# Decoder layer with mixture of experts: low halves of the down weights and routing weights made on VectorE in place of GpSimd

## The chip, the cores and the metric

The kernel runs on one core of one Trainium2 chip. The metric is the device time of one execution in microseconds (us), by the median of several runs. In the text PE is TensorE, DVE is VectorE, ACT is ScalarE, POOL is GpSimd and SP is SyncE, which here only issues DMA loads. L1710 is line 1710 of the kernel before; in the changed kernel lines after L1659 stand one lower (L1711).

## What is computed

One decoder layer for 1024 tokens of 1024 float32 values: attention by two mixers, attention over a memory, and a mixture of 16 experts, of which each token uses 2. The change is in the last of these:

```python
combine = jnp.sum(jax.nn.one_hot(expert_id, N_EXPERTS, dtype=jnp.float32) * w_sel[..., None], axis=-2)
y = jnp.zeros(h.shape, jnp.float32)
for e in range(N_EXPERTS):
    act = jax.nn.silu(h @ w_gate[e]) * (h @ w_up[e])
    y = y + combine[..., e:e + 1] * (act @ w_down[e]).astype(jnp.float32)
return y.astype(h.dtype)
```

`w_gate` and `w_up` are 1024 x 256 per expert, `w_down` is 256 x 1024. The kernel computes only the rows that an expert was chosen for.

## The kernel before

Matmuls are exact to about float32 by halves: every operand is split into a high half (made on ACT, `hi`) and a low half (`lo` = operand minus `hi`), and `mm3` (L520 to L522) adds three products, hi x hi, hi x lo and lo x hi. So each weight tile costs one ACT instruction and one subtraction for its halves before PE can use it.

Before the experts, the rows of all tokens are scattered in DRAM into a table `d_xs`, sorted by expert, with four extra values per row (two routing weights, an expert's number, the token). `moe` then goes over the experts in the order of their size, small (96 or 128 rows) and big (160 to 224 rows, two blocks of up to 128) in turn. For each expert:

- `load` / `rows_in` (L1631) puts on SP's queue the loads of the rows, `xg`, and of the extra values, `emore`.
- `tokens` / `rows_of` (L1652) makes for each block of 128 rows the token number `etok` (L1661) and the routing weight `ewt` (L1663 to L1666) in five small POOL instructions, and transposes the rows on PE into `eT`, split into halves (L508, DVE, for the low one).
- `gate_up` (L1691) loads gate and up weights in two halves of two tiles each into `gu_raw` (two buffers), makes `gu_hi` on ACT (L1698) and `gu_lo` on DVE (L1699). Four gu_lo of 128 x 1024 that follow on each other are called a burst here.
- `first_big` or `first_small` is the first pair of products, with silu and `ea`; its result `aT` is again split in halves (`aT_hi` on ACT, `aT_lo` on DVE).
- `down` (L1703) loads the two halves of the down weights into `dn_raw` (two buffers, L1707), makes `dn_hi` on ACT (L1709) and `dn_lo` (L1710) on the engine `E`, POOL by default.
- `second` (L1721) multiplies by the down weights, scales by `ewt` while copying out of PSUM (`ey`, ACT, L1730, two buffers) and adds the rows to the output in DRAM by an indirect DMA of POOL (`result`, L1716), the scatter. Each scatter waits until the one before has landed. There are 24 of them.

`ewt` and `etok` have four buffers each, so the etok of a new expert can be written only when the scatter of an expert four places earlier has read its own, that is, when it has landed. The order on each engine's queue is not that of the program's text: a scheduler sets it from its own estimate of times, so a change of engine moves other instructions too. Every queue runs in order: an instruction that waits holds all behind it.

The two parts that the change touches are the engine G (POOL) in L1661 to L1666 and the call

```python
            dn = down(i, expert[i])
```

in the loop (L1839). Two of the 16 experts are handled ahead of the loop, with `early` blocks of 128 rows.

Of the kernel before, what the change touches and what calls it, by code (L numbers as in the profile page):

```python
# [14 lines left out]
OP = mybir.AluOpType  # L15
# [4 lines left out]
S, D, T, KD = 1024, 1024, 8, 8  # L20
# [469 lines left out]
class Hybrid:  # L490
# [1119 lines left out]
    def moe(self, route):  # L1610
        tc, nc, I = self.tc, self.nc, self.I
        V, G, A = nc.vector, nc.gpsimd, nc.scalar
# [39 lines left out]
        def rows_of(loaded, exf, eT, early=False):  # L1652


            n, xg, more, _ = loaded
            wt, tok = (rt.tile([128, *sh], dt, name=nm, bufs=4) for nm, sh, dt in (("ewt", (2, 2), F32), ("etok", (2,), I32)))
            for b in range(0, n, 128):
                m, b_ = min(128, n - b), b // 128
                mo, w = more[0:m, b_], wt[0:m, b_]  # L1659
                with tc.issue_after(route.puts[-1].ins) if early else nullcontext():  # L1660
                    G.tensor_scalar(tok[0:m, b_:b_ + 1], mo[:, 3:4], float(S), None, op0=OP.add)  # L1661

                    G.tensor_scalar(w[:, 1:2], mo[:, 2:3], exf if isinstance(exf, float) else exf[0:m], None, op0=OP.is_equal)  # L1663
                    G.tensor_sub(w[:, 0:1], mo[:, 0:1], mo[:, 1:2])
                    G.tensor_mul(w[:, 0:1], w[:, 0:1], w[:, 1:2])
                    G.tensor_add(w[:, 0:1], w[:, 0:1], mo[:, 1:2])  # L1666
            for b in range(0, n, 128):
                m = min(128, n - b)
                x = xg[0:m, b // 128].rearrange("p (c i) -> p c i", c=KD)
                for k in range(0, KD, 4):  # L1670
                    p = self.tp().rearrange("p (c j) -> p c j", c=4)
                    for c in range(4):
                        nc.tensor.transpose(p[:, c, 0:m], x[:, k + c], self.ident[0:m, 0:m])
                    self.split(*(h[:, k:k + 4, b:b + m] for h in eT), p[:, :, 0:m])
            return *eT, wt, tok

        def weights(nm, ex, pat, **kw):
            return I[nm][0, slice(ex, ex + 1) if isinstance(ex, int) else ds(ex, 1)].rearrange("o " + pat, **kw)
# [12 lines left out]
        def gate_up(m, ex, halves, E=V, raws=None):  # L1691

            ws = []
            for h in halves:
                raw = raws[h] if raws else gate_up_in(m, ex, h)
                hi, lo = (p.tile([128, 2, 4, 256], F32R, name=f"gu_{w}{h}") for w, p in zip(("hi", "lo"), (((rx, rx), (rx, e01)), ((e2, e2), (e01, ry)))[m % 2][h]))
                for z, raw_z in enumerate(raw):
                    A.activation(hi[:, z], raw_z, AF.Copy)  # L1698
                    E.tensor_sub(lo[:, z], raw_z, hi[:, z].bitcast(F32))  # L1699
                ws += [(hi[:, :, i], lo[:, :, i]) for i in range(4)]  # L1700
            return ws

        def down(i, ex, E=G):  # L1703
            dn = []
            for f in range(2):
                raw = ra.tile([128, D], F32, name="dn_raw", bufs=2)
                ends[2] = nc.sync.dma_start(raw, weights('moe_w_down', ex, "(f p) d -> (o f) p d", f=2)[f])  # L1707
                hi, lo = (((e01, e01), (ry, r1))[i % 2][f].tile([128, D], F32R, name=f"dn_{w}{f}") for w in ("hi", "lo"))
                A.activation(hi, raw, AF.Copy)  # L1709
                E.tensor_sub(lo, raw, hi.bitcast(F32))  # L1710
                dn.append((hi, lo))  # L1711
            return dn
# [8 lines left out]
        def second(n, aT, dn, wt, tok):  # L1721
            for b in range(0, n, 128):
                y, m_ = r3.tile([128, D], F32, name="ey", bufs=2), min(128, n - b)
                t = slice(b, b + m_)
                for h in range(2):
                    ps = self.acc()
                    m = slice(h * 512, (h + 1) * 512)
                    for f in range(2):
                        self.mm3(ps[0:m_], (aT[f][0][:, t], aT[f][1][:, t]), (dn[f][0][:, m], dn[f][1][:, m]), f == 0, f == 1)
                    ends[0] = A.activation(y[0:m_, m], ps[0:m_], AF.Copy, scale=wt[0:m_, b // 128, 0:1])  # L1730
                ends[1] = result(y[0:m_], tok[0:m_, b // 128:b // 128 + 1])
# [44 lines left out]
        def early(i, ex, exf):  # L1776

            a = (r3 if i else ra).tile([128, D], F32, name="ey" if i else "dn_raw", bufs=2)
            h, l = (eT[i][0][:, z * 1024:z * 1024 + 1024] for z in range(2))
            return rows_of(rows_in(128, ex, 0, xg3(a), True), exf, [cut(w, 128) for w in (h, l)], True)  # L1780

        gu = gate_up(0, 0, (0, 1), G)
        dn = down(0, 0)
# [7 lines left out]
        expert, loaded = [0, lead[0], lead[1]], {}  # L1791

        def load(k):
            if k < NE:
                n, r = (ROOM[k] - 128, 128) if k < 2 else (ROOM[ORDER_[k]], 0)
                if k > 2:
                    with tc.issue_after(loaded[k - 1][3].ins):
                        expert.append(nc.values_load(nb[0:1, 16 + ORDER_[k]:17 + ORDER_[k]], engines=SP, min_val=0, max_val=NE - 1))
                loaded[k] = rows_in(n, expert[k], r, xg3(xg_[k % 3]))

        def tokens(k):
            n, exf = loaded[k][0], (0.0, route.le[:, 0:1])[k] if k < 2 else route.ex[:, ORDER_[k]:ORDER_[k] + 1]
            return n, rows_of(loaded[k], exf, [cut(w, n) for w in eT[k % 2]])
# [27 lines left out]
        for i in range(2, NE):  # L1831
            if i + 1 < NE:
                load(i + 2)
                gu1 = gate_up(i + 1, expert[i + 1], (0,))
                n1, hT1 = tokens(i + 1)
            rest = (first_big if n > 128 else first_small)(n, gu, hT)
            if i + 1 < NE:
                gu = gu1 + gate_up(i + 1, expert[i + 1], (1,), V)
            dn = down(i, expert[i])  # L1839
            second(*last)  # L1840
            last = (n, rest(), dn, *hT[2:])
            if i + 1 < NE:
                n, hT = n1, hT1
# [102 lines left out]
```

## Time and profile before

| | us |
|---|---|
| median of 3 runs | 1425.78 |
| lowest, highest | 1419.15, 1425.79 |
| profiled execution | 1426.21 |
| its span, first to last instruction | 1424.4 |
| loop over experts within the span | about 1185 to 1415 |
| busy in the span: PE, DVE, ACT, POOL | 1249.4, 887.7, 808.0, 596.9 |
| granted clock of PE, mean | 0.948 of full speed |

Read such a profile from the stage that a change touches, not from the sums of the span: an engine with a low share can hold up the others in its own stage, and one with a high share may be waited for by nobody. A row of waits names the instruction that sat idle, what ended its idle time, the total, the count and the longest one.

### The profile page before, as it was taken

Reading aid. Unit: us, or ns where it says so; the run is one execution under the profiler, and the core shown is the slowest. Engines: PE = TensorE matmul, PEld = TensorE weight load, DVE = VectorE, ACT = ScalarE, POOL = GpSimd, SP = SyncE. Lnnn points to the kernel's source line nnn. Section 1 sums busy time; section 2 is a strip of 40 time slices with the busy share of each in tenths; the row PEclk is TensorE's granted clock in tenths of the full one; section 3 lists DMA queues with packets and bytes.
Section 4 is the critical chain, followed back from the end, with each engine's and each line's share of the span. In section 5 each row is a group of like instructions: output and inputs, shape, how many; then the busy total and the mean of one; then the engine's idle time right before and its main releaser. Section 6 shows DMA issues by size and latency. Waiting matters only on the chain.

```text
span 1424.4 us, 20689 instructions
## 1 busy us (share of the span) xinstructions
PE 1249.4 (88%) x6876; PEld 1043.0 (73%) x6877; DVE 887.7 (62%) x1699; ACT 808.0 (57%) x1671; POOL 596.9 (42%) x723
## 2 busy tenths in 40 slices
PE   5798799988999999999988999999996378989894
PEld 4677688777777778888777787887885367778772
DVE  5542765889999578788978465132258854545550
ACT  5553554886662388889988322044453346556552
POOL 6897200527884121211343222012335445556652
PEclk9999899998999999999999999998998799999987
DMA  7555002534334554435221244421113779888872
GB/s 211 146 162 157 29 20 74 155 115 145 128 120 149 158 162 149 168 139 186 62 82 52 83 133 145 162 69 38 47 58 119 262 232 313 261 249 267 236 238 36
DMA packets 145605, 203.54 MB, mean 143 GB/s; under 512 B 69808, under 2 KB 91056, under 8 KB 145488
## 3 DMA queue, kind: packets, MB, share of 16 engines
q1 hardware_dynamic: 136896, 173.22, 38.2%
q0 software_dynamic: 7440, 24.71, 6.5%
q10 hardware_dynamic: 1152, 4.19, 0.7%
q8 instruction: 56, 0.92, 0.3%
q14 instruction: 61, 0.50, 0.1%
HBM read 134.61 MB, written 69.70 MB: 143 GB/s over the span
## 4 chain that ended last, share of the span: by engine, by line
PE 48%; DVE 14%; DMA 10%; ACT 10%; issue 8%; POOL 6%; SPq 0%; ACTq 0%; POOLq 0%; DVEq 0%
PE acc L520 6%; PE acc L521 6%; PE acc L522 6%; PE s L520 4%; PE s L522 4%; PE s L521 4%; DMA dn_raw<-in_moe_w_down_dram 2%; DMA gu_raw<-in_moe_w_up_dram 2%; ACT tk_junka L1178 2%; PE tp L1334 2%; PE s L911 2%; PE tp L1431 1%; PE s L1414 1%; DMA out_dram<-ey,etok 1%; DMA gu_raw<-in_moe_w_gate_dram 1%
## 5 line engine op out<-in xcount | busy, mean ns | idle before, releaser
L512 POOL TENSOR_TENSOR wl<-wr,wh 128x512 fp32r<-128x512 f32 (+2 forms) x94 | 119.5, 1286 | 145.6 <-ACT wh L511 109.7
L1699 DVE TENSOR_TENSOR gu_lo<-gu_raw,gu_hi 128x1024 fp32r<-128x1024 f32 x60 | 80.6, 1365 | 71.0 <-ACT gu_hi L1698 69.0
L508 DVE TENSOR_TENSOR PT_lo<-tp,PT_hi 128x512 fp32r<-128x512 f32 x152 | 101.6, 685 | 26.2 <-ACT PT_hi L507 24.9
L520 PE MATMUL s<-hT_hi,wh 128*128 128x512 f32 x256 | 102.6, 401 | 3.4 <-ACT s L1039 3.4
L522 PE MATMUL s<-hT_hi,wl 128*128 128x512 f32 x256 | 101.6, 399 | 1.6 <-POOL wl L512 1.6
L511 ACT ACTIVATE wh<-wr 128x512 fp32r<-128x512 f32 (+2 forms) x94 | 55.7, 610 | 82.3 <-PE acc L522 29.5
L521 PE MATMUL s<-hT_lo,wh 128*128 128x512 f32 x256 | 101.4, 399 | 0.0
L507 ACT ACTIVATE PT_hi<-tp 128x512 fp32r<-128x512 f32 x152 | 86.9, 594 | 20.4 <-PE tp L1431 8.7
L1178 ACT ACTIVATE tk_junka<-sc,tk_b 128x512 bf16<-128x512 f32 (+2 forms) x96 | 79.4, 827 | 29.9 <-DVE tk_b L1175 29.0
L1710 POOL TENSOR_TENSOR dn_lo<-dn_raw,dn_hi 128x1024 fp32r<-128x1024 f32 x32 | 80.5, 2519 | 31.2 <-ACT dn_hi L1709 28.0
L520 PE MATMUL acc<-wh,hT_hi 128*128 128x512 f32 (+2 forms) x240 | 86.6, 362 | 3.6 <-ACT hT_hi L507 1.5
L522 PE MATMUL acc<-wh,hT_lo 128*128 128x512 f32 (+2 forms) x240 | 85.8, 357 | 1.6 <-DVE hT_lo L508 1.6
L521 PE MATMUL acc<-wl,hT_hi 128*128 128x512 f32 (+2 forms) x240 | 85.9, 358 | 0.6 <-POOL wl L512 0.6
L1698 ACT ACTIVATE gu_hi<-gu_raw 128x1024 fp32r<-128x1024 f32 x60 | 61.7, 1052 | 36.9 <-DMA gu_raw<-in_moe_w_gate_dram 26.2
L529 POOL TENSOR_TENSOR rq_y<-ms,mhalf 128x11 f32<-128x11 f32 (+3 forms) x29 | 71.8, 2482 | 0.7
L1316 DVE TENSOR_REDUCE low<-s 128x1 f32<-128x256 f32 (+3 forms) x64 | 49.1, 769 | 32.8 <-PE s L1315 32.5
L1716 POOL DMA_INDIRECT out_dram<-ey,etok x24 | 40.3, 1681 | 63.9 <-ACT ey L1730 47.2
L520 PEld LDWEIGHTS s<-hT_hi,wh 128*128 128x128 f32 x256 | 49.3, 193 | 13.8 <-ACT s L1039 4.2
L522 PEld LDWEIGHTS s<-hT_hi,wl 128*128 128x128 f32 x256 | 49.2, 192 | 11.9 <-POOL wl L512 2.1
L521 PEld LDWEIGHTS s<-hT_lo,wh 128*128 128x128 f32 x256 | 49.4, 193 | 10.1
L920 DVE SCALAR_TENSOR_TENSOR sc<-rel,iw,sc 128x384 f32<-128x384 f32 (+5 forms) x42 | 42.2, 1004 | 22.5 <-ACT rel L914 19.3
L520 PE MATMUL s<-eT1h,gu_hi 128*128 128x224 f32 (+2 forms) x192 | 54.3, 283 | 1.8 <-ACT eT1h L507 1.8
(529 smaller groups left out, 4171.7 us busy)
## 6 DMA issues: line engine op xcount, KB each, us to landing
d_xs<-zero SPq DMA_DIRECT2D x32, 516.0 KB
dn_raw<-in_moe_w_down_dram SPq DMA_DIRECT2D x32, 512.0 KB
gu_raw<-in_moe_w_gate_dram SPq DMA_DIRECT2D x30, 512.0 KB
gu_raw<-in_moe_w_up_dram SPq DMA_DIRECT2D x30, 512.0 KB
wr<-in_w_in_dram SPq DMA_DIRECT2D x48, 256.0 KB
d_g<-s SPq DMA_DIRECT2D x32, 256.0 KB
gt<-d_g SPq DMA_DIRECT2D x16, 512.0 KB
xg<-d_xs SPq DMA_DIRECT2D x13, 512.0 KB
```

What stands on the lines that cost most here:

```text
L507: self.nc.scalar.activation(hi, src, AF.Copy)
L508: self.nc.vector.tensor_sub(lo, src, hi.bitcast(F32))
L511: self.nc.scalar.activation(hi, src, AF.Copy)
L512: self.nc.gpsimd.tensor_sub(lo, src, hi.bitcast(F32))
L520: mm(out, a[0], b[0], start=start, stop=False)
L521: mm(out, a[0], b[1], start=False, stop=False)
L522: mm(out, a[1], b[0], start=False, stop=stop)
L529: nc.gpsimd.tensor_tensor(y, v, self.mhalf.to_broadcast([128, n]), op=OP.pow)
L1178: A.activation(junka[:, :(t + 1) * 128], blk(t), AF.Sign, bias=b[:, i:i + 1].bitcast(F32), accum_out=cnt[:, i:i + 1])
L1698: A.activation(hi[:, z], raw_z, AF.Copy)
L1699: E.tensor_sub(lo[:, z], raw_z, hi[:, z].bitcast(F32))
L1710: E.tensor_sub(lo, raw, hi.bitcast(F32))
```

## The change

`rows_of` makes etok and ewt on DVE instead of POOL, except in the two early blocks, which stay on POOL: 22 blocks of five instructions move. `down` in the loop is called with DVE: 28 of the 32 dn_lo move, four (the two experts ahead of the loop) stay. Loads, products, sizes and buffers are as before.

```diff
@@ -1657,13 +1657,14 @@
+                E = G if early else V
                 with tc.issue_after(route.puts[-1].ins) if early else nullcontext():
-                    G.tensor_scalar(tok[0:m, b_:b_ + 1], mo[:, 3:4], float(S), None, op0=OP.add)
+                    E.tensor_scalar(tok[0:m, b_:b_ + 1], mo[:, 3:4], float(S), None, op0=OP.add)
...
@@ -1836,7 +1837,7 @@
-            dn = down(i, expert[i])
+            dn = down(i, expert[i], V)
```

The lines for ewt change in the same way as the one for etok.

The order of instructions moves with it. First place: DVE at the burst of gu_lo that begins at 1218.18 us in the profile before. Names carry buffer numbers; in brackets stand the semaphores waited for, DMASW being those of POOL's scatters, which take turns over eight, and DMAHW those of loads. Before:

```order
L1746 TENSOR_TENSOR ea<-ea,s 128x224 [waits Activation_49]
L508 TENSOR_TENSOR aT_lo<-ea,aT_hi 128x224 [waits Activation_49]
L1699 TENSOR_TENSOR gu_lo_12477<-gu_raw,gu_hi_12476 128x1024 [waits DMAHW2_49,PE_49,Activation_49]
L1699 TENSOR_TENSOR gu_lo_12477<-gu_raw,gu_hi_12476 128x1024 [waits DMAHW3_49,Activation_49]
L508 TENSOR_TENSOR eT1l<-tp,eT1h 128x4x128 [waits Activation_49]
L1699 TENSOR_TENSOR gu_lo_12554<-gu_raw,gu_hi_12553 128x1024 [waits DMAHW4_49,PE_49,Activation_49]
L1699 TENSOR_TENSOR gu_lo_12554<-gu_raw,gu_hi_12553 128x1024 [waits DMAHW5_49,Activation_49]
```

After:

```order
L1662 TENSOR_SCALAR etok<-emore 128x1 [waits DMASW2_49]
L1662 TENSOR_SCALAR etok<-emore 96x1
L1667 TENSOR_TENSOR ewt<-ewt,emore 128x1 [waits DVE_49]
L1711 TENSOR_TENSOR dn_lo_12562<-dn_raw,dn_hi_12561 128x1024 [waits DMAHW6_49,Activation_49]
L1711 TENSOR_TENSOR dn_lo_12568<-dn_raw,dn_hi_12567 128x1024 [waits DMAHW7_49,PE_49,Activation_49]
L1662 TENSOR_SCALAR etok<-emore 128x1 [waits DMASW3_49]
L1700 TENSOR_TENSOR gu_lo_12477<-gu_raw,gu_hi_12476 128x1024 [waits DMAHW2_49,PE_49,Activation_49]
L1700 TENSOR_TENSOR gu_lo_12477<-gu_raw,gu_hi_12476 128x1024 [waits DMAHW3_49,Activation_49]
L508 TENSOR_TENSOR eT1l<-tp,eT1h 128x4x128 [waits Activation_49]
L1700 TENSOR_TENSOR gu_lo_12554<-gu_raw,gu_hi_12553 128x1024 [waits DMAHW4_49,PE_49,Activation_49]
L1700 TENSOR_TENSOR gu_lo_12554<-gu_raw,gu_hi_12553 128x1024 [waits DMAHW5_49,Activation_49]
```

Two dn_lo and the last ewt now stand ahead of the burst, and an etok with a wait for DMASW3, the fifth of the 24 scatters. In the later part of the loop there are etok with such a wait ahead of three more bursts or inside them. POOL's queue holds in this stretch only the scatters.

Second place: ACT at the gate load of a big expert's successor (gu_hi_12999, at 1262.34 us before). Before:

```order
L507 ACTIVATE eT1h<-tp 128x4x128 [waits PE_49]
L1756 ACTIVATE ea<-x 128x256 [waits DVE_49,PE_49]
L1698 ACTIVATE gu_hi_12999<-gu_raw 128x1024 [waits DMAHW6_49]
L507 ACTIVATE aT_hi<-ea 128x224 [waits DVE_49]
L507 ACTIVATE eT1h<-tp 128x4x64 [waits PE_49] x2
L1698 ACTIVATE gu_hi_12999<-gu_raw 128x1024 [waits DMAHW7_49]
```

After:

```order
L507 ACTIVATE eT1h<-tp 128x4x128 [waits PE_49]
L1757 ACTIVATE ea<-x 128x256 [waits DVE_49,PE_49]
L507 ACTIVATE aT_hi<-ea 128x224 [waits DVE_49]
L1699 ACTIVATE gu_hi_12999<-gu_raw 128x1024 [waits DMAHW6_49]
L507 ACTIVATE eT1h<-tp 128x4x64 [waits PE_49]
L1699 ACTIVATE gu_hi_12999<-gu_raw 128x1024 [waits DMAHW7_49]
L507 ACTIVATE eT1h<-tp 128x4x64 [waits PE_49]
```

The aT_hi of the big expert (224 rows) stood behind a gu_hi that waits for its load, and now stands ahead of it.

Third place: ACT two big experts later (gu_hi_13717). Before:

```order
L1756 ACTIVATE ea<-x 128x256 [waits DVE_49,PE_49]
L507 ACTIVATE aT_hi<-ea 128x192 [waits DVE_49]
L507 ACTIVATE eT1h<-tp 128x4x32 [waits PE_49]
L1698 ACTIVATE gu_hi_13717<-gu_raw 128x1024 [waits DMAHW2_49]
L507 ACTIVATE eT1h<-tp 128x4x32 [waits PE_49]
L1698 ACTIVATE gu_hi_13717<-gu_raw 128x1024 [waits DMAHW3_49]
```

After:

```order
L1757 ACTIVATE ea<-x 128x256 [waits DVE_49,PE_49]
L1699 ACTIVATE gu_hi_13717<-gu_raw 128x1024 [waits DMAHW2_49]
L507 ACTIVATE eT1h<-tp 128x4x32 [waits PE_49]
L507 ACTIVATE aT_hi<-ea 128x192 [waits DVE_49]
L1699 ACTIVATE gu_hi_13717<-gu_raw 128x1024 [waits DMAHW3_49]
L507 ACTIVATE eT1h<-tp 128x4x32 [waits PE_49]
```

Here the aT_hi (192 rows) stood ahead of the gu_hi and now stands behind it. The same is found once more, at the next big expert (gu_hi_14074).

## Rows read from the trace of the kernel before

**Rows 1.** The page, part 1: busy us, share of the span, instructions of each engine.

```profile
PE 1249.4 (88%) x6876; PEld 1043.0 (73%) x6877; DVE 887.7 (62%) x1699; ACT 808.0 (57%) x1671; POOL 596.9 (42%) x723
```

**Rows 2.** Two 20-us windows: busy us (count) by engine, PEclk, DMA share, GB/s.

```profile
1200.00:1220.00 20.00, 19.28 (x141) 17.38 (x142) 7.36 (x12) 11.87 (x19) 16.74 (x25) 1.00 0.89 248
1260.00:1280.00 20.00, 16.27 (x94) 14.01 (x95) 9.25 (x13) 12.51 (x21) 8.49 (x11) 0.83 1.01 325
```

**Rows 3.** Waits of SP's queue, 1185 to 1425: total us, times, longest.

```profile
SPq L1688 <- DVE gu_lo L1699: 53.3, 12, 9.5
SPq L1707 <- POOL dn_lo L1710: 32.9, 15, 5.4
```

**Rows 4.** DVE in order of time: start, us, instruction, idle before and releaser.

```profile
1218.18 4.58 DVE L1699 TENSOR_TENSOR gu_lo<-gu_raw,gu_hi 128x1024 fp32r<-128x1024 f32 x2 [6.29 <-ACT gu_hi L1698]
...
1251.48 3.61 DVE L1699 TENSOR_TENSOR gu_lo<-gu_raw,gu_hi 128x1024 fp32r<-128x1024 f32 x2 [8.10 <-ACT gu_hi L1698]
...
1285.32 2.36 DVE L1699 TENSOR_TENSOR gu_lo<-gu_raw,gu_hi 128x1024 fp32r<-128x1024 f32 x2 [6.35 <-ACT gu_hi L1698]
...
1314.40 3.73 DVE L1699 TENSOR_TENSOR gu_lo<-gu_raw,gu_hi 128x1024 fp32r<-128x1024 f32 x2 [9.03 <-ACT gu_hi L1698]
...
1346.58 3.72 DVE L1699 TENSOR_TENSOR gu_lo<-gu_raw,gu_hi 128x1024 fp32r<-128x1024 f32 x2 [9.82 <-ACT gu_hi L1698]
...
1380.92 6.84 DVE L1699 TENSOR_TENSOR gu_lo<-gu_raw,gu_hi 128x1024 fp32r<-128x1024 f32 x4 [1.34 <-ACT gu_hi L1698]
```

**Rows 5.** Waits of PE, 1185 to 1415.

```profile
PE acc L520 <- ACT aT_hi L507: 10.2, 6, 4.4
...
PE acc L521 <- POOL dn_lo L1710: 1.0, 1, 1.0
```

**Rows 6.** POOL by lines, 1185 to 1415: count, busy us, mean ns, idle before.

```profile
L1710 POOL TENSOR_TENSOR dn_lo<-dn_raw,dn_hi 128x1024 fp32r<-128x1024 f32 x28 | 71.1, 2541 | 22.5 <-ACT dn_hi L1709 19.3 <-DMA xg<-d_xs 2.7
L1716 POOL DMA_INDIRECT out_dram<-ey,etok x23 | 38.7, 1681 | 57.2 <-ACT ey L1730 40.5 <-DMA out_dram<-ey,etok 8.5 <-ACTq L1854 5.2
L1661 POOL TENSOR_SCALAR etok<-emore 128x1 int32<-128x1 f32 (+3 forms) x19 | 9.6, 503 | 13.6 <-DMA out_dram<-ey,etok 12.5
L1663 POOL TENSOR_SCALAR ewt<-emore,ex_f 128x1 f32<-128x1 f32 (+3 forms) x19 | 9.1, 500 | 3.0 <-ACT ey L1730 3.0
L1664 POOL TENSOR_TENSOR ewt<-emore 128x1 f32<-128x1 f32 (+3 forms) x19 | 5.8, 324 | 0.0
L1666 POOL TENSOR_TENSOR ewt<-ewt,emore 128x1 f32<-128x1 f32 (+3 forms) x19 | 5.3, 399 | 0.6
L1665 POOL TENSOR_TENSOR ewt<-ewt 128x1 f32<-128x1 f32 (+3 forms) x19 | 3.7, 208 | 0.5
```

**Rows 7.** DMA strip, 1214 to 1227 in 40 steps: GB/s.

```profile
GB/s 340 328 366 429 429 403 416 304 140 114 66 39 1 140 51 63 88 76 101 113 101 13 0 0 0 0 0 0 0 0 139 227 328 265 290 202 315 227 340 340
```

**Rows 8.** POOL in order of time, near one burst and in the tail.

```profile
1216.19 1.51 POOL L1716 DMA_INDIRECT out_dram<-ey,etok  x1 [0.17 <-DMA dn_raw<-in_moe_w_down_dram]
...
1218.35 3.33 POOL L1710 TENSOR_TENSOR dn_lo<-dn_raw,dn_hi 128x1024 fp32r<-128x1024 f32 x1
...
1402.58 2.86 POOL L1710 TENSOR_TENSOR dn_lo<-dn_raw,dn_hi 128x1024 fp32r<-128x1024 f32 x1
1405.61 1.44 POOL L1716 DMA_INDIRECT out_dram<-ey,etok  x1 [0.17 <-issue]
```

**Rows 9.** A small instruction of DVE, in order of time.

```profile
1145.32 0.16 DVE L261 TENSOR_TENSOR cb<-cb,ex_s 1x16 f32<-1x16 f32 x1
```

**Rows 10.** Waits of POOL, 1185 to 1415.

```profile
POOL etok L1661 <- DMA out_dram<-ey,etok: 12.5, 4, 5.3
POOL out_dram L1716 <- DMA out_dram<-ey,etok: 8.5, 4, 3.3
```

**Rows 11.** The scatter's line, 1185 to 1425: from issue to landing.

```profile
DMA to landing us min/median/max: 3.0/8.9/11.7
```

**Rows 12.** ACT in order of time, where it waits for a gate load.

```profile
1262.34 1.06 ACT L1698 ACTIVATE gu_hi<-gu_raw 128x1024 fp32r<-128x1024 f32 x1 [6.22 <-DMA gu_raw<-in_moe_w_gate_dram]
```

More of the change, by code (lines that the diff above doesn't have):

```diff
@@ L1659, in rows_of @@
                 mo, w = more[0:m, b_], wt[0:m, b_]
+                E = G if early else V
                 with tc.issue_after(route.puts[-1].ins) if early else nullcontext():
-                    G.tensor_scalar(tok[0:m, b_:b_ + 1], mo[:, 3:4], float(S), None, op0=OP.add)
[L1663 to L1666, printed above, removed]
+                    E.tensor_scalar(tok[0:m, b_:b_ + 1], mo[:, 3:4], float(S), None, op0=OP.add)
+                    E.tensor_scalar(w[:, 1:2], mo[:, 2:3], exf if isinstance(exf, float) else exf[0:m], None, op0=OP.is_equal)
+                    E.tensor_sub(w[:, 0:1], mo[:, 0:1], mo[:, 1:2])
+                    E.tensor_mul(w[:, 0:1], w[:, 0:1], w[:, 1:2])
+                    E.tensor_add(w[:, 0:1], w[:, 0:1], mo[:, 1:2])
             for b in range(0, n, 128):
```

## Prediction

> **What bounds the kernel now.** I read the page's busy shares first, then only the stretch that the change touches: the loop over experts, about 1185 to 1415 us. Over the whole span POOL looks idle (42%) beside PE with 88% [rows 1]; shares of the span say nothing about one stage. By 20-us windows the loop has two nearly full resources at once [rows 2]: PE is busy 19.28 of 20 us in the first window shown with a DMA share of 0.89, and 16.27 of 20 in the second with DMA at 1.01 and a granted clock of 0.83. DVE works 7 to 9 of those 20 us, POOL 8 to 17. So neither engine named in the change is full; it can pay only by what it holds up. Three such hold-ups can be seen. First, SP's queue waits 32.9 us in 15 places for a POOL dn_lo before it may issue the next dn_raw load, but longer, 53.3 us in 12, for DVE's gu_lo [rows 3]. Second, DVE's gu_lo gets slower whenever POOL's dn_lo runs beside it: a pair takes 2.36 us alone, and 4.58, 3.61, 3.73 and 3.72 us in four of the places where the two meet, and four in a row take 6.84 where two free pairs would be 4.72 [rows 4]. Third, PE itself hardly waits for POOL (1.0 us, once); its largest wait is 10.2 us for aT_hi of ScalarE [rows 5].
>
> **Part 1, dn_lo to VectorE.** Taken off POOL: 28 instructions, 71.1 us, 2.54 each [rows 6]. Put on DVE: 28 at half a free pair, 1.18 us, so 33 us. DVE's load of 7 to 9 us in 20 rises by about 3; I cost this work itself at nothing where it stands in DVE's idle time before a burst of gu_lo (6 to 10 us of idle stand in front of all bursts shown but the last [rows 4]). Where the second dn_raw lands just ahead of the burst, its dn_lo now stands in front of gu_lo in DVE's queue (the excerpt of DVE's order): between 0 and a pair, 2.4 us, per burst. I take 0.4, near the low end, because gu_lo must wait for ScalarE's gu_hi anyway and dn_hi stands ahead of gu_hi there: five bursts, +2.0 (0 to +12).
> What is gained is the meeting of the two engines: (4.58 + 3.61 + 3.73 + 3.72) - 4 x 2.36 = 6.2, and 6.84 - 4.72 = 2.1 for the four in a row, together -8.3 us. This counts in full, since the end of a burst frees gu_raw, which SP waits for longest [rows 3], and since the DMA rate falls to nothing around it: in the strip of 40 steps from 1214 to 1227 us (0.325 us each) it falls from over 400 GB/s to 0, and stays there for eight steps or 2.6 us before the next loads come [rows 7]. The other end is 0, if PE, nearly full, does not notice the loads coming earlier.
> Here a rule can be set against the rows. At 1218.35 POOL's dn_lo took 3.33 us where the mean is 2.54, and DVE's pair beside it was 2.2 us too long [rows 4, 6, 8]: both pay. The Trainium skill, SBUF — State Buffer, section "Who interferes with whom", says that a VectorE instruction with two SBUF inputs and a GpSimd instruction that reads SBUF lock each other out, the second to issue waiting until the first is done. By that, each of five meetings costs DVE at most one whole dn_lo; five at the listed mean of 2.54 would make the gain 12.7 where the rows give 8.3. The sum below would then end at 1419.5 in place of 1423.9. The rows are lower, as POOL is at times the one that waits, and I go by them.
>
> **Part 2, routing weights and tokens to VectorE.** Each of 19 blocks in the stretch has five small instructions on POOL: 9.6 + 9.1 + 5.8 + 5.3 + 3.7 = 33.5 us [rows 6]. DVE does an operation of this size in 0.16 us [rows 9]: 95 x 0.16 = 15 us of busy time, in idle time, so nothing by themselves. The wait they bring is not nothing. etok's buffer is released by the landing of an earlier scatter, and on POOL that cost 12.5 us of waiting in 4 places, with nothing but POOL's own work behind it [rows 10]. DVE's queue is in order, too: behind etok now stand gu_lo, aT_lo and eT1l, for which SP, PE and the next transposes wait. In the first excerpt, etok waits for the fifth scatter just ahead of a burst. That scatter starts at 1216.19 [rows 8], and its traffic is gone from the DMA strip shortly after 1221 [rows 7], so gu_lo, which began at 1218.18, would begin up to 3.2 us later. Three later bursts have an etok with such a wait ahead of them or inside them, for scatters that end about when the burst begins: a median scatter lands in 8.9 us (3.0 to 11.7), and the next waits for it by up to 3.3 [rows 10, 11]. I take +1 for each: 3.2 + 3 = +6.2. Bounds: 0, if POOL, free of other work, issues each scatter earlier, and the whole 12.5 us.
>
> **Part 3, what the order does elsewhere.** One 4.4-us wait of PE was for an aT_hi that ScalarE had put behind a gu_hi waiting 6.22 us for its load [rows 5, 12]. The change puts that aT_hi ahead of the gu_hi; two big experts later it does the reverse (second and third excerpts). I take -4.4 for the first and +2.2, half of it, for each of two places of the other kind, which sums to 0; bounds -4.4 (no new stall) to +4.4 (both as long as the old one). With each stall the granted clock goes as well: 0.83 in the window of the old one [rows 2], which at 20 us is 3.4 us of full-speed work. I put no sum to that, as one is lost and others may come.
>
> **Part 4, the tail.** After the last load PE waits 1.0 us for a POOL dn_lo [rows 5], and the scatter at 1405.61 starts when POOL is done with a dn_lo begun at 1402.58 that took 2.86 [rows 8]; on DVE it would be 1.7 shorter. Nothing hides the tail: -1.0 and, as the ey it scatters may be late by itself, -1.2 of the 1.7 (0 to -2.7).
>
> **Sum.** -8.3 + 2.0 + 6.2 + 0 - 2.2 = -2.3 us. The profiled execution was 1426.2, 0.4 above the median of the runs (1425.8; the lowest 1419.2). So 1423.9, taken as **1423.5 us**, which is within 0.5% (7.1 us, about what a measurement of this kernel can tell from no change) of before.
>
> **Rivals.**
> - *POOL was feeding the loads.* If every dn_lo that is 1.36 us shorter lets its successor's load go that much sooner, 14 experts with a chain of one such step each give -19, less the 2 of part 1, so 1409 with no etok waits, and 1415 with those of part 2. For it: SP's 32.9 us [rows 3], and meetings gone. Against it: DMA at 0.89 to 1.01 [rows 2]; a load that is issued sooner queues behind others. Chance 0.34 (1404 to 1418).
> - *VectorE's queue takes the scatters' waits.* One mechanism: etok stands in front of a burst until a scatter has landed. It decides from the point where the waits before bursts pass the 8.3 + 2.2 us that the parts above give. At the full 12.5 us and the 8.5 of one scatter waiting for the other [rows 10], with part 1 at +2: 1426.2 - 10.5 + 2 + 21 = 1438.7; the third excerpt's aT_hi stalls would add 4. For it: the order excerpts; against it: DVE is idle for over half of the time, and POOL, left with 38.7 us of scatters [rows 6], issues them earlier. Chance 0.25 (1433 to 1440).
> - *The change does nothing that counts*: loads fill the DMA and PE fills the rest, so a burst that ends earlier is followed by a longer wait for the load. Then 1426; it lies inside my forecast's case, whose chance is 0.41 with it (1419 to 1433).
>
> **How the numbers follow.** Faster by over 0.5% is the first rival, 0.34; slower is the second, 0.25; the rest, 0.41, is within 0.5%. The likeliest case alone runs from 1419 to 1433. The range that should hold 8 in 10 takes in most of both rivals: 1408 to 1437.
>
> **What would show it right or wrong.** Right: gu_lo pairs at 2.4 us everywhere and a mean under 1.25; dn_lo on DVE at about 1.2; POOL's busy time in the loop near 39 us; etok on DVE with waits for out_dram of 4 to 8 us in all; bursts of gu_lo that begin up to 3 us later in the first place. Wrong towards faster: SP's wait for dn_lo under 15 us, and PE busy over 19 of 20 in most windows. Wrong towards slower: etok waits over 10 us with gu_lo behind them, or new PE waits for aT_hi of 4 us with the clock at 0.83 or lower in more windows than before.

## The result and the profile after

| | us |
|---|---|
| before, median of 11 runs (lowest, highest) | 1422.36 (1418.2, 1426.58) |
| changed, median of 11 runs (lowest, highest) | 1434.83 (1428.69, 1437.48) |
| ratio, 95% interval | 1.0081 (1.0064 to 1.0099) |
| profiled execution of the changed kernel, its span | 1428.69, 1426.8 |

The change makes the kernel slower by 0.8%, some 11.5 us (0.81% of 1422.36). The forecast was no change (-2.3 us); the rival with 0.25, "VectorE's queue takes the scatters' waits", is what happened. Its price (1438.7) was near partly by luck: it counts 21 us of waits in full and a gain of 10.5 less 2, where 36.1 us of waits and a gain of 3.7 were measured (below).

The profiled execution of the changed kernel is also the fastest of its 11, so its span is only 2.4 us longer than that of the kernel before. The extra time is in the stage all the same. An instruction shortly before it is a mark common to both. The kernel before, DVE in order of time:

```profile
1145.51 2.39 DVE L262 CAST nb<-cb 1x16 int32<-1x16 f32 x1
```

The changed kernel, the same instruction:

```profile
1139.98 2.41 DVE L262 CAST nb<-cb 1x16 int32<-1x16 f32 x1
```

From this mark to the end of the span it takes 278.9 us before (1424.4 - 1145.51) and 286.8 after (1426.8 - 1139.98): 7.9 us more in the stage, while what lies ahead of the mark was 5.5 us shorter in this execution. I use this measure below only beside ratios, since it comes from one execution each.

Beside rows 1, the page of the changed kernel: busy times (part 1) and the shares of the chain that ended last (part 4).

```profile
PE 1244.9 (87%) x6876; PEld 1039.1 (73%) x6877; DVE 915.5 (64%) x1837; ACT 809.1 (57%) x1671; POOL 495.2 (35%) x585
...
PE 44%; DVE 15%; DMA 14%; ACT 10%; issue 9%; POOL 5%; SPq 0%; POOLq 0%; DVEq 0%; ACTq 0%
DMA out_dram<-ey,etok 7%; PE acc L520 5%; PE acc L521 5%; PE acc L522 5%; PE s L520 3%; PE s L522 3%; PE s L521 3%; ACT tk_junka L1178 2%; DMA dn_raw<-in_moe_w_down_dram 2%; PE tp L1334 2%; PE s L911 2%; DVE ik_hi L1168 1%; DVE ik_lo L1168 1%; PE acc L1348 1%; PE acc L1347 1%
```

In the chain the landing of scatters (out_dram<-ey,etok) has 7% of the span; before it had 1%, as this line of the page before shows:

```profile
PE acc L520 6%; PE acc L521 6%; PE acc L522 6%; PE s L520 4%; PE s L522 4%; PE s L521 4%; DMA dn_raw<-in_moe_w_down_dram 2%; DMA gu_raw<-in_moe_w_up_dram 2%; ACT tk_junka L1178 2%; PE tp L1334 2%; PE s L911 2%; PE tp L1431 1%; PE s L1414 1%; DMA out_dram<-ey,etok 1%; DMA gu_raw<-in_moe_w_gate_dram 1%
```

DVE by lines in the changed kernel, 1185 to 1420 us, beside rows 4 and 6:

```profile
L1700 DVE TENSOR_TENSOR gu_lo<-gu_raw,gu_hi 128x1024 fp32r<-128x1024 f32 x48 | 57.4, 1219 | 7.6 <-ACT gu_hi L1699 7.5
L1711 DVE TENSOR_TENSOR dn_lo<-dn_raw,dn_hi 128x1024 fp32r<-128x1024 f32 x28 | 34.2, 1222 | 24.8 <-ACT dn_hi L1710 24.7
...
L1664 DVE TENSOR_SCALAR ewt<-emore,ex_f 128x1 f32<-128x1 f32 (+3 forms) x17 | 3.4, 205 | 10.6 <-ACT ey L1731 10.6
...
L1662 DVE TENSOR_SCALAR etok<-emore 128x1 int32<-128x1 f32 (+3 forms) x19 | 2.4, 146 | 25.5 <-DMA out_dram<-ey,etok 25.5
```

gu_lo now takes 1219 ns on the mean. The shortest and longest of all 60 are 1204 and 1228 ns, where the longest was 3435 before, so the meetings of rows 4 are gone. That is what the Trainium skill's rule on the two engines' lock (SBUF — State Buffer, "Who interferes with whom") leads one to expect, and here rows and rule agree. dn_lo takes 1222 ns, half of POOL's 2541 [rows 6], and the small instruction 146. The price stands in the last column of etok and ewt: 25.5 and 10.6 us of DVE's queue standing still. The waits of PE and of DVE, 1185 to 1415 us, beside rows 5 and 10:

```profile
PE tp L1674 <- DVE eT1l L508: 15.1, 5, 6.2
PE acc L520 <- ACT aT_hi L507: 3.8, 4, 2.1
PE tp L1764 <- DVE eT1l L508: 3.4, 2, 2.8
```

```profile
DVE etok L1662 <- DMA out_dram<-ey,etok: 25.5, 8, 6.0
...
DVE ewt L1664 <- ACT ey L1731: 10.6, 5, 3.9
```

PE no longer waits for POOL, and its wait for aT_hi fell from 10.2 to 3.8 us; its wait for eT1l grew to 15.1 and 3.4 us, from 3.6 and 1.2 in the same stretch. SP's waits, 1185 to 1425, beside rows 3:

```profile
SPq L1689 <- DVE etok L1662: 16.3, 2, 10.6
...
SPq L1708 <- DVE ewt L1665: 13.3, 5, 4.8
SPq L1708 <- DVE dn_lo L1711: 6.1, 3, 2.7
```

SP's wait for dn_lo fell from 32.9 to 6.1 us, which the prediction had named as a sign of a faster kernel; waits for etok and ewt took its place. Two places show how a scatter gets to PE. DVE in order of time:

```profile
1295.45 0.15 DVE L1662 TENSOR_SCALAR etok<-emore 128x1 int32<-128x1 f32 x1 [5.96 <-DMA out_dram<-ey,etok]
1295.52 0.41 DVE L1758 TENSOR_TENSOR ea<-ea,x 128x256 f32<-128x256 f32 x1
1295.85 0.42 DVE L508 TENSOR_TENSOR eT1l<-tp,eT1h 128x256 fp32r<-128x256 f32 x1
1296.18 1.22 DVE L1700 TENSOR_TENSOR gu_lo<-gu_raw,gu_hi 128x1024 fp32r<-128x1024 f32 x1
...
1319.88 1.22 DVE L1700 TENSOR_TENSOR gu_lo<-gu_raw,gu_hi 128x1024 fp32r<-128x1024 f32 x1
1325.86 0.15 DVE L1662 TENSOR_SCALAR etok<-emore 128x1 int32<-128x1 f32 x1 [4.76 <-DMA out_dram<-ey,etok]
1325.94 1.23 DVE L1700 TENSOR_TENSOR gu_lo<-gu_raw,gu_hi 128x1024 fp32r<-128x1024 f32 x1
...
1327.34 0.68 DVE L508 TENSOR_TENSOR eT1l<-tp,eT1h 128x512 fp32r<-128x512 f32 x1
```

At 1289.5 DVE came to an etok whose buffer an earlier scatter still held, and stood for 5.96 us; ea, eT1l and gu_lo waited behind it, none of which has to do with the scatter. At 1321.1 the same happened inside a burst of gu_lo, for 4.76 us, and then PE, which needed the eT1l behind it:

```profile
1321.49 0.43 PE L1674 MATMUL tp<-ident,xg 32*128 32x32 f32 x4
1328.08 0.63 PE L1674 MATMUL tp<-ident,xg 32*128 32x32 f32 x4 [6.17 <-DVE eT1l L508]
```

The chain of the changed kernel, in order of time, has both scatters:

```profile
1284.84 10.59 DMA out_dram<-ey,etok
...
1295.52 0.14 DVE ea L1758
...
1317.52 8.32 DMA out_dram<-ey,etok
...
1325.94 0.17 DVE gu_lo L1700
```

10.59 and 8.32 us of the path are the landing of a scatter. Before, POOL waited for such landings too [rows 10], but only POOL's work was queued there.

### The profile page after: what moved, and what is told of

Its sections match the earlier page's. It is cut to its first block, busy times and chain, and to the rows that moved or that the text cites. A ratio compares the mean times of both kernels' runs of the same rounds, so it can differ in the third digit from the quotient of the medians.

```text
span 1426.8 us, 20677 instructions
## 1 busy us (share of the span) xinstructions
PE 1244.9 (87%) x6876; PEld 1039.1 (73%) x6877; DVE 915.5 (64%) x1837; ACT 809.1 (57%) x1671; POOL 495.2 (35%) x585
## 4 chain that ended last, share of the span: by engine, by line
PE 44%; DVE 15%; DMA 14%; ACT 10%; issue 9%; POOL 5%; SPq 0%; POOLq 0%; DVEq 0%; ACTq 0%
DMA out_dram<-ey,etok 7%; PE acc L520 5%; PE acc L521 5%; PE acc L522 5%; PE s L520 3%; PE s L522 3%; PE s L521 3%; ACT tk_junka L1178 2%; DMA dn_raw<-in_moe_w_down_dram 2%; PE tp L1334 2%; PE s L911 2%; DVE ik_hi L1168 1%; DVE ik_lo L1168 1%; PE acc L1348 1%; PE acc L1347 1%
## 5 line engine op out<-in xcount | busy, mean ns | idle before, releaser
L1700 DVE TENSOR_TENSOR gu_lo<-gu_raw,gu_hi 128x1024 fp32r<-128x1024 f32 x60 | 71.9, 1220 | 14.5 <-ACT gu_hi L1699 14.4
L520 PEld LDWEIGHTS acc<-wh,hT_hi 128*128 128x128 f32 x240 | 46.5, 194 | 12.0 <-ACT ev L744 2.7
```

Of the source, the lines that this page charges most:

```text
L520: mm(out, a[0], b[0], start=start, stop=False)
```

## The experiments

Ratios are to the kernel before, timed on the same chip in the same rounds. Where two runs' orders are compared, I count, from the mark above to the end and without the five small instructions, how many of the 236 instructions of ACT, 189 of DVE and 1328 of PE (by tile and shape, in order of time) stand outside the longest order that both share. The runs are told in the order of the questions. All of them:

| run | dn_lo on | etok, ewt on | buffers | further | ratio (95%) |
|---|---|---|---|---|---|
| the change | DVE | DVE | 4 | | 1.0081 (1.0064 to 1.0099) |
| e1_dn_lo_only | DVE | POOL | 4 | | 0.9974 (0.9955 to 0.9993) |
| e2_rows_only | POOL | DVE | 4 | | 1.0063 (1.0039 to 1.0087) |
| e3_bufs8 | DVE | DVE | 8 | | 1.0021 (1.0002 to 1.0039) |
| e4_etok_pool | DVE | ewt DVE, etok POOL | 4 | | 1.0006 (0.9989 to 1.0023) |
| e5_dn_lo_bufs8 | DVE | POOL | 8 | | 0.9975 (0.9958 to 0.9992) |
| e6_before_bufs8 | POOL | POOL | 8 | | 1.0008 (0.9991 to 1.0025) |
| e7_bufs3 | DVE | DVE | 3 | | 1.0039 (1.0019 to 1.0060) |
| e8_rows_bufs8 | POOL | DVE | 8 | | 1.0057 (1.0038 to 1.0076) |
| e9_pinned | DVE | DVE | 4 | small ones tied behind dn_lo | 1.0035 (1.0018 to 1.0051) |
| e12_dn_lo_aT | DVE | POOL | 4 | gu_hi tied behind aT_hi | 0.9949 (0.9934 to 0.9965) |
| e13_pinned_aT | DVE | DVE | 4 | both of these ties | 1.0012 (0.9987 to 1.0037) |
| e14_before_aT | POOL | POOL | 4 | gu_hi tied behind aT_hi | 0.9994 (0.9976 to 1.0013) |
| e15_dn_lo_dup | DVE | POOL, again on DVE unread | 4 | | 1.0043 (1.0019 to 1.0066) |
| e16_dn_lo_dup2 | DVE | POOL, twice on DVE unread | 4 | | 1.0015 (0.9996 to 1.0035) |
| e17_pinned_ties | DVE | DVE | 4 | as e13, gu_hi also behind eT1h | 1.0044 (1.0027 to 1.0062) |
| e19_dn_lo_ties | DVE | POOL | 4 | gu_hi behind aT_hi and eT1h | 1.0026 (1.0011 to 1.0042) |
| e20_after_ties | DVE | DVE | 4 | gu_hi behind aT_hi and eT1h | 1.0115 (1.0096 to 1.0134) |

**Which part of the change costs?** dn_lo alone (edit against the kernel before), and the small instructions alone (edit against the changed kernel):

```diff
-            dn = down(i, expert[i])
+            dn = down(i, expert[i], V)
```

> Only the 28 dn_lo go to VectorE; etok and ewt stay on GpSimd. Theory (etok's and ewt's waits in VectorE's queue are the loss): faster than before by 4 to 8 us, a ratio of 0.994 to 0.997, gu_lo at about 1.22 us each. Rival A (a dn_lo ahead of each burst on VectorE delays gu_lo, and that is the loss): slower by 6 to 13 us, 1.004 to 1.009.

```diff
-            dn = down(i, expert[i], V)
+            dn = down(i, expert[i])
```

> Only etok and ewt go to VectorE; dn_lo stays on GpSimd. Theory: slower than before by 10 to 20 us, 1.007 to 1.014, with 20 us or more of etok waiting on scatters and PE waiting over 10 us for eT1l. Rival A: within 4 us of before, 0.997 to 1.003.

dn_lo alone is faster by 0.26%, a little short of the 0.3 to 0.6% that the theory asked for; the small instructions alone are slower by 0.63%, just under the theory's 0.7. The rival that a dn_lo ahead of a burst costs the time has fallen. In e2 DVE waits 17.2 us for scatters, where 20 or more were expected, and 10.7 for ey.

**Is it the wait, and which?** More buffers, and etok alone back on POOL:

```diff
-            wt, tok = (rt.tile([128, *sh], dt, name=nm, bufs=4) for nm, sh, dt in (("ewt", (2, 2), F32), ("etok", (2,), I32)))
+            wt, tok = (rt.tile([128, *sh], dt, name=nm, bufs=8) for nm, sh, dt in (("ewt", (2, 2), F32), ("etok", (2,), I32)))
```

> The whole change, with eight buffers in place of four for etok and ewt, so that neither has to wait for a scatter or an ey of four experts earlier. Theory: etok and ewt wait under 3 us in all, and the time is 4 to 8 us under before, 0.994 to 0.997. Rival A: as the change, 1.006 to 1.010. Rival B (the order on ScalarE and TensorE that the scheduler makes, aT_hi behind a waiting gu_hi, is the loss): 1.004 to 1.010 with PE waits for aT_hi of over 8 us.

```diff
-                    E.tensor_scalar(tok[0:m, b_:b_ + 1], mo[:, 3:4], float(S), None, op0=OP.add)
+                    G.tensor_scalar(tok[0:m, b_:b_ + 1], mo[:, 3:4], float(S), None, op0=OP.add)
```

> The whole change, but etok (22 instructions) stays on GpSimd; ewt and dn_lo are on VectorE. Theory: the 25 us of waits for scatters leave VectorE's queue, ewt's 10 us for ey stay; 3 us under before to 3 above, 0.998 to 1.002. Rival A: as the change, 1.006 to 1.010.

Eight buffers give back 0.6 of the 0.8%, and etok on POOL 0.75; that second run lies where the theory put it. It is also the cleanest of all: its orders are all but those of the change (4 instructions stand elsewhere on ACT, 4 on DVE, 11 on PE), and etok waits almost as long as there, only on POOL. Waits of POOL in e4_etok_pool, 1185 to 1425:

```profile
POOL etok L1662 <- DMA out_dram<-ey,etok: 23.2, 5, 7.2
```

In the same stretch PE's waits for eT1l are 1.8 and 0.6 us, where the change has 15.1 and 3.4. So the same wait costs 0.75%, 10.7 us, more on DVE's queue than on POOL's, in very nearly the same order; the two intervals lie apart, and etok's own work there is 2.4 us.

But eight buffers were expected at 0.994 to 0.997 and came to 1.0021: with no waits for scatters left, 0.5% over dn_lo alone remained. Something else had changed with them: PE now waited 14.1 us for eT1h from ACT, where the change has 0.7.

**Do buffers help by themselves, and does a longer wait cost more?** Four runs: e5 is e1, e6 the kernel before and e8 is e2 with eight buffers; e7 is the change with three.

> dn_lo alone on VectorE, and eight buffers for etok and ewt, which stay on GpSimd. If GpSimd's waits of 21 us for scatters and 19 us for ey still held up scatters in the run with dn_lo alone: 0.993 to 0.996. If they cost nothing there (GpSimd has nothing urgent behind them): as that run, 0.996 to 0.999.

> The kernel before with eight buffers for etok and ewt. If the 12.5 us that etok waits on GpSimd cost dn_lo behind it: 0.994 to 0.997. If those waits are covered there: 0.998 to 1.002.

> The whole change with three buffers for etok and ewt in place of four, so that each waits for the scatter and the ey of three experts earlier: the suspected wait is made longer. Theory: over 35 us of such waits in VectorE's queue, and 1.012 to 1.025. Rival B (the loss is the order on ScalarE and TensorE, not the wait): 1.005 to 1.010, as with four.

> Only etok and ewt go to VectorE, with eight buffers; dn_lo stays on GpSimd. Theory: no waits for scatters or ey are left in VectorE's queue, so most of the 0.6% that the same move cost with four buffers is gone: 0.998 to 1.003. If the 110 small instructions cost by themselves: 1.004 to 1.007.

In the kernel before the waits on POOL cost nothing: e6 has 0.2 us of them in place of 12.5 and 3.0, almost no instruction in another place (1 on ACT, 2 on PE), and the same time (1.0008). e5 beside e1 (0.9975 and 0.9974) cannot tell, as its waits on POOL did not go; e1's 21.4 us for scatters and 18.8 for ey gave way to this one (POOL's waits in e5_dn_lo_bufs8, 1185 to 1425):

```profile
POOL etok L1661 <- DMA emore<-d_xs: 34.6, 6, 9.3
```

Two expectations failed. Three buffers did not lengthen the wait: DVE waited 23.5 us in 7 places for scatters and 11.2 in 5 for ey, about as with four, and the run was even faster than the change. So the sum of the waits is no measure of the loss; PE's longest wait for eT1l was 2.2 us there, where the change has 6.2, and the order moved too (18, 9 and 87). And with eight buffers, but dn_lo on POOL, the loss stayed (1.0057): etok now stood in front of its own load there and waited 11.0 us for emore, up to 8.8 at once. Both would fit one reason, which I read off the order of instructions and which no run tests: the scheduler puts etok about where it believes the buffer, or the load, to be ready; with fewer buffers that is later, with more it is earlier. The depth moves the place of the wait and hardly its length.

**The place, then.** The five small instructions are made when they are used, and tied to a place where the scatter of four experts earlier has long landed (cut from the edit):

```diff
+            pin = [q for d, q in pins if d is dn][0]
+            with tc.issue_after(pin.ins):
+                wt, tok = route_rows()
```

(`pins` holds the last dn_lo of each expert, `route_rows` the five instructions per block as before.)

> The whole change with four buffers, but the five small instructions of an expert are tied behind the last dn_lo of the same expert on VectorE, so that the scatter of four experts earlier has long landed when etok comes up; no other edit. Theory (etok's and ewt's waits in VectorE's queue are the loss): these waits under 4 us in all, and 0.995 to 0.999, as with dn_lo alone. Rival A (the work itself on VectorE): 1.004 to 1.010.

The waits are gone, and 0.46% with them; 1.0035 is still 0.6% over e1, though, and between what the two theories said.

**What holds back dn_lo alone, and the rest?** In e1 PE waits 14.6 us for aT_hi, in the trace of which the reason can be seen. e1_dn_lo_only, ACT in order of time:

```profile
1249.42 1.06 ACT L1698 ACTIVATE gu_hi<-gu_raw 128x1024 fp32r<-128x1024 f32 x1 [2.33 <-DMA gu_raw<-in_moe_w_gate_dram]
1250.38 0.36 ACT L1756 ACTIVATE ea<-x 128x256 f32<-128x256 f32 x1
1252.89 1.06 ACT L1698 ACTIVATE gu_hi<-gu_raw 128x1024 fp32r<-128x1024 f32 x1 [2.15 <-DMA gu_raw<-in_moe_w_up_dram]
1253.85 0.37 ACT L507 ACTIVATE aT_hi<-ea 128x224 fp32r<-128x224 f32 x1
1254.13 0.64 ACT L507 ACTIVATE eT1h<-tp 128x256 fp32r<-128x256 f32 x2
1255.28 1.06 ACT L1698 ACTIVATE gu_hi<-gu_raw 128x1024 fp32r<-128x1024 f32 x1 [0.51 <-DMA gu_raw<-in_moe_w_gate_dram]
```

and what PE does meanwhile:

```profile
1254.28 0.79 PE L520 MATMUL acc<-dn_hi,aT_hi 128*128 128x512 f32 x1 [4.20 <-ACT aT_hi L507]
```

The aT_hi that PE needs stands behind gu_hi that wait for loads. A tie is to put it in front, in three runs (cut from the edit; `ahi` lists the aT_hi of the big experts as they are made):

```diff
+                ahi.append(A.activation(aT[f][0], a, AF.Copy))
...
-                gu1 = gate_up(i + 1, expert[i + 1], (0,))
+                with tc.issue_after(ahi[-1].ins) if ahi and n > 128 else nullcontext():
+                    gu1 = gate_up(i + 1, expert[i + 1], (0,))
```

> dn_lo alone on VectorE, and on ScalarE the gu_hi of a big expert's successor are tied behind the aT_hi that they held up (four places in the run with dn_lo alone, 3.2 to 4.2 us of TensorE's waiting each or 2.75). If those waits were the reason that dn_lo alone gave 0.26% and not the 0.6% of the prediction's parts 1 and 4: 0.990 to 0.995, TensorE's waits for aT_hi under 5 us. If the loads set the pace: 0.996 to 0.999.

> Both ties together, with the whole change. If the small instructions cost nothing on VectorE once they don't wait: within 0.002 of the run with dn_lo alone and the tie on ScalarE. If they cost: 0.003 or more above it.

> The kernel before with the tie on ScalarE alone. Its one wait of 4.4 us for aT_hi and several of 1 to 2 go: 0.995 to 0.998 if they were on the path, 0.999 to 1.001 if the loads set the pace.

ACT in order of time in e12_dn_lo_aT, the same place:

```profile
1257.53 0.39 ACT L1748 ACTIVATE aT_hi<-ea 128x224 fp32r<-128x224 f32 x1 [1.45 <-DVE ea L1747]
1258.78 1.06 ACT L1698 ACTIVATE gu_hi<-gu_raw 128x1024 fp32r<-128x1024 f32 x1 [0.86 <-DMA gu_raw<-in_moe_w_gate_dram]
```

The aT_hi is in front, but the tie does not say so itself. When it is set, the last aT_hi listed is that of the big expert two places back, and what it ties are the first two gu_hi of the expert after the current one. In e1 these already stood behind that aT_hi: the one at 1255.28 and its next, which PE's products of the small expert use from 1269.73 on, before any later gu_hi is made. The gu_hi that held it up, at 1249.42 and 1252.89, are the second half of the current big expert's own, so neither the expectation nor the heading of the second place ahead of the prediction, "a big expert's successor", names them rightly. That these moved too is what the scheduler made of the tie, and not they alone: 26 instructions stand elsewhere than in e1 on ACT, 22 on DVE and 87 on PE.

With dn_lo on DVE the tie brings 0.9949, the best of all runs, faster than both kernels by more than their intervals, though its interval just overlaps that of e1; PE's waits for that aT_hi fell from 14.6 to 5.4 us, a little over the 5 expected. With dn_lo on POOL the same tie is worth nothing that can be told (0.9994). With the small instructions on DVE (e13) 0.6% more is paid than in e12.

**Is it their work on DVE?** The small instructions run on POOL for use, and on DVE again, into tiles that nobody reads (cut from the edit, which also gives emore, that they read, six buffers in place of four):

```diff
+                with tc.issue_after([q for d, q in pins if d is dn][0].ins):
+                    f()
```

> As the run with dn_lo alone on VectorE, etok and ewt made on GpSimd; in addition the 110 small instructions run on VectorE too, tied behind dn_lo of the same expert, into tiles that nobody reads. If their presence in VectorE's queue costs the missing half (16 us of work, of which about 8 on the path): 1.002 to 1.005. If it is that ey and the scatters depend on VectorE: 0.996 to 0.999, as with dn_lo alone.

> The same with the unread small instructions twice on VectorE, 220 in all. Presence: 1.006 to 1.012. Dependence: 0.996 to 1.000.

Done once for nothing they cost as much as when they are used (1.0043): it is not that ey or the scatters depend on DVE. Done twice they do not cost more (1.0015, outside both ranges expected), so it is not their time either. What else the unread instructions move is the scheduler's order. The orders of e15 on ACT, DVE and PE are those of e9 to the last instruction; e16 (2 on ACT and 8 on PE elsewhere) and e3 (5 on ACT, 1 on DVE, 48 on PE) come near it, and e1 does not (22, 13 and 113). In e15 eT1h stands on ACT behind a gu_hi that waits for its load, ahead of aT_hi. PE's waits in e15_dn_lo_dup, 1185 to 1425 us:

```profile
PE s L520 <- ACT eT1h L507: 12.9, 7, 4.2
...
PE acc L520 <- ACT aT_hi L507: 1.7, 1, 1.7
```

In e1 the first of these was 3.1 us; in e9, e16 and e3 it is 11.6, 16.4 and 14.1. So the loss over e1 that e3, e9, e15 and e16 share (1.0015 to 1.0043, where e1 has 0.9974) goes with this order and these waits. That the order alone is the reason is argued: no run has it without small instructions on DVE. So ACT's order was fixed next, by tying the gu_hi behind eT1h as well (cut from the edit):

```diff
+                with ExitStack() as tie:
+                    if n > 128:
+                        for q in ahi[-1:] + ehi[-1:]:
+                            tie.enter_context(tc.issue_after(q.ins))
...
```

> The whole change with the small instructions tied behind dn_lo, and on ScalarE the gu_hi tied behind aT_hi and behind the last eT1h. If the order on ScalarE was the other half of the loss: within 0.002 of the same ties with dn_lo alone, 0.993 to 0.998. If it is the work in VectorE's queue: 0.004 to 0.007 above that run.

> dn_lo alone on VectorE, with both ties on ScalarE. As the run with the tie of aT_hi alone or a little under it, 0.992 to 0.996, with TensorE's waits for aT_hi and eT1h under 4 us in all.

> The change as it is (etok and ewt free to wait), with both ties on ScalarE. The waits of 25 us for scatters stay: 0.004 to 0.007 above the run with the small instructions tied, 1.000 to 1.007.

The second tie itself was a bad idea: e19 is 0.8% slower than e12, not a little faster. SP's waits for gu_lo grew. e12_dn_lo_aT and e19_dn_lo_ties, 1185 to 1425:

```profile
SPq L1688 <- DVE gu_lo L1699: 58.6, 13, 9.4
```

```profile
SPq L1692 <- DVE gu_lo L1703: 73.7, 14, 10.7
```

A gu_hi that is held back holds its gu_raw, and SP cannot load the next: 73.7 us in place of 58.6. That this is the reason is not shown; e5 waits 74.6 us in the same row, at 0.9975, and the order of e19 differs from that of e12 in much (43 instructions on ACT, 34 on DVE, 128 on PE). e17 and e19 compare more fairly (11, 6 and 35). e17 over e19 is 0.18%: the small instructions, when they wait for nothing, cost 2.5 us there of the 13 us that they take in the change, and the intervals of the two runs overlap. e20 over e17 is 0.71%, or 10 us. By design only the place of etok and ewt differs, but the scheduler's order went with it (40, 22 and 140), so this pair shows less than the change beside e4. DVE's waits in e20_after_ties:

```profile
DVE etok L1664 <- DMA out_dram<-ey,etok: 37.4, 11, 9.3
...
DVE ewt L1666 <- ACT ey L1736: 7.1, 4, 3.6
```

37.4 and 7.1 us of waiting, more than in the change itself, and the slowest of all runs.

## Why the prediction was wrong, step by step

- *What bounds the kernel*: borne out as far as the waits show. Neither DVE nor POOL was full, and the change was paid for in waits of PE (eT1l) and of SP (etok, ewt).
- *Part 1*: the meetings of the two engines went, as forecast. Parts 1 and 4 summed to -8.3 + 2.0 - 2.2 = -8.5 us. dn_lo alone measured -0.26%, -3.7 us, and -0.51%, -7.2 us, in e12, where an aT_hi no longer stood behind a waiting gu_hi. So the size was about right if the difference of these two runs, whose intervals just overlap, is the order on ScalarE, which part 3 took to sum to 0; e12 moves other instructions as well.
- *Part 2 is the step that failed*: "etok waits for the fifth scatter just ahead of a burst ... I take +1 for each: 3.2 + 3 = +6.2", with 12.5 us as the upper bound. Measured were 25.5 us in 8 places, and 10.6 in 5 places for ewt behind ey, of which the row of POOL [rows 6, ewt L1663] showed 3.0 and the prediction said nothing. The bound was wrong in kind: 12.5 us is what POOL waited with its own late queue, and a queue that arrives earlier waits longer for the same landing (POOL itself waits 21.4 us in e1, where dn_lo is gone from it). Also, the longest waits were not at the bursts that I looked at, but in front of eT1l and inside a burst, where nothing stands between DVE and PE. In time, etok's wait on DVE costs 0.75%, 10.7 us, by the change over e4, which differs in little else; the change over e9 gives 0.46%, 6.5 us, with more of the order moved (14, 9 and 59). All that part 2 stands for, the change over e1, is 1.07% or 15 us, where +6.2 was forecast.
- *The small instructions' own work, costed at nothing*: within 0.2% by e17 over e19, whose intervals overlap, and in e16 twice the work cost no more than once.
- *Part 3*: the one 4.4-us wait for aT_hi went, and the two feared ones were smaller (2.1 us the longest). "Sums to 0" was close for the change. That a tie on ScalarE can move the time by up to 0.8% (e19 over e12) was not foreseen.
- *Part 4*: PE's wait for dn_lo in the tail went. The scatters at the end hardly came sooner: from the third-last to the last it took 10.6 us before (1401.68 to 1412.30) and 10.4 in the changed kernel (1404.20 to 1414.61), as each now waits for the landing before it. Of the -1.2 forecast there at most 0.2 is seen.
- *The sign*: with the waits at their measured length, part 2 alone outweighs part 1. The slower rival had that as its deciding point, and I gave it 0.25 because DVE is idle for half of the time. Idle time does not help against a wait in an in-order queue: it is a mean, and the instruction behind the wait is late whatever the mean.

Not settled: what the 0.32% between e1 and e4 is made of (the waits of ewt, 9.7 us on DVE in e4, and 19, 11 and 90 instructions in other places), and whether the order that e3, e9, e15 and e16 share costs by itself.

## What to carry to other kernels

A small instruction that reuses a buffer held by a DMA may stand only on a queue where nothing urgent is behind it: on GpSimd some 15 us of such waits cost nothing (e6), and 23.2 us of them there (e4) cost 10.7 us less than 25.5 us on VectorE. Moving work off a slow engine should be decided operation by operation (here the large one pays, the small ones do not), and where a scheduler sets the order, price what it does to the other queues or tie it down; more buffers alone took only part of the loss away here, and nothing of it with dn_lo on GpSimd. The version to keep is dn_lo alone on VectorE with aT_hi ahead of the gu_hi: 0.9949.

## What was not expected of the hardware

Nothing in the single instructions: 2.54 us on GpSimd became 1.22 on VectorE, and 0.2 to 0.5 us became 0.15 to 0.2. New was how far the landing of a scatter lies from its issue, and how unevenly: 7.8 us in the median after, 8.9 before [rows 11], and from 3.3 to 10.9 us after, so that nothing placed by one expected landing time can be right for all.
